# Norm scale folded into the up projection's weight rows, chunks of 1024 columns, and no weight halves on GpSimd: a hybrid decoder layer on one Trainium2 core

## The chip, the cores and the metric

The kernel runs on one core of a Trainium2 chip. The metric is the device time of one launch in microseconds (us), the median over several runs; lower is better. Five engines matter: TensorE (PE in the profile, its weight loads PEld), VectorE (DVE), ScalarE (ACT), GpSimd (POOL) and SyncE (SP), whose queue issues the weight transfers.

## The reference

One decoder layer in float32 on 256 tokens of width 2048. All of it must be computed; the part that the change touches is the last quarter of it:

```python
x = x + _rmsnorm(mixed @ w_out[layer], norm_attn_post[layer])      # 2048 -> 2048

h = _rmsnorm(x, norm_mlp_pre[layer])                               # x / rms(x) * gain
u = jnp.square(jax.nn.relu(h @ w_up[layer]))                       # 2048 -> 8192
x = x + _rmsnorm(u @ w_down[layer], norm_mlp_post[layer])          # 8192 -> 2048
```

`mixed` is what two groups of attention heads give (a dilated sliding window, and a latent attention); it is not touched.

## The kernel before

**Arithmetic.** Each float32 operand of a large product is split into two parts, `hi` and `lo`: ScalarE copies the value to the rounded type (`hi`, line 235), and another engine subtracts that from the value (`lo`, line 236). A product is then three matmuls of 128x128 by 128x512: hi·hi, hi·lo and lo·hi. The activations (`hT`, transposed, 128 tokens a block) are the stationary operand, the weights the moving one; `tok(hT[x], k, b)` is the block `b` (0 or 1) of tokens at row block `k` of 16.

**Weights.** The class `Weights` streams all weights in tiles of 128x1024 through SyncE's queue into 5 `raw` buffers; each is split into one of 8 pairs of `hi` and `lo` buffers. `get(i)` writes the instructions for tiles up to `ahead` = 6 beyond tile `i` into the program (4 while the residual below runs). The `lo` parts are on VectorE, but for three tiles of the first up chunk (`POOL_U = (3, 5, 7)`), which are on GpSimd.

**Order.** Every engine runs its instructions in the order in which the program writes them. The class `Flow` sets that order: `spend` adds a planned duration for each matmul (0.2158 us, `MM`) and transpose (0.109 us, `TR`) to a planned clock; side work is a generator (a "chain") that yields the planned delay until its next step; `pump`, called after each group of three matmuls, writes the steps that have come due. So the place of a transpose among the matmuls is fixed beforehand; if its input or its bank is late, TensorE waits there.

**From the output projection to the up projection.** When the last chunk of the output projection is done for a block `b`, `residual(b)` starts (the second block 4.0 us later in the plan, `D_SECOND`): the sum of squares, the scale `rstd_post` (GpSimd), then `update`: x += yg·rstd (line 646) and yg = x·g_pre2 (line 649) by quarters of 512 columns; after a planned 4.5 us (`D_NORM`) four steps, 1.5 us apart, each transposing a quarter of yg into a bank `ht` (2 banks, tag `tp`) and splitting it into `hT`. The factor 1/rms is not in `hT`; it comes as `rstd2[b]` when the up projection's sums are read out.

**Up projection.** 16 chunks `j` of 512 columns; each has 8 weight tiles of two row blocks (`K2`), and per tile and block 6 matmuls. The first chunk takes 7 tiles for block 0 first, then the same 7 for block 1 (`APART[1]` = 7), all else alternates between the blocks. A chunk has two accumulators (one 512-column bank per block, out of 4 with the tag `acc`). When a block's accumulator is complete, ScalarE writes r = relu(acc·rstd2) (line 739) into one of 2 buffers `r`, and a chain `up_evac` follows:

```python
    def up_evac(j, b, r):
        yield D_UP + b * 0.7                       # D_UP = 2.0
        t = tp_bank(f"rt{j}_{b}")                  # tag tp, 2 banks
        for k in range(4):
            transpose(t[:, k * P:(k + 1) * P], r[:, k * P:(k + 1) * P])
        nc.scalar.activation(uT[j][:, :, b * P:(b + 1) * P], t.rearrange("p (k s) -> p k s", k=4), AF.Square)
```

The delay counts from the first `pump` after the chain was started. A tile of `r` is free for the next one when its four transposes are done; a bank of `tp` when line 714 (uT) has read it.

**Down projection.** 16 groups of 4 row blocks with tiles of 1 x 1024 columns and 8 accumulators (all banks), then the last norm and the output.

Of the kernel before, what the change touches and what calls it, by code (L numbers as in the profile page):

```python
# [26 lines left out]
P = 128  # L27
# [43 lines left out]

RAW_BUFS, W_BUFS, W_AHEAD, AHEAD_NORM = 5, 8, 6, 4
POOL_U = (3, 5, 7)

APART = (5, 7)

# [62 lines left out]
class Weights:  # L142


    def __init__(self, nc, pool, split, bufs, ahead):
        self.nc, self.pool, self.split_fn = nc, pool, split
        self.bufs, self.limit, self.ahead = bufs, bufs, ahead
        self.specs, self.tiles, self.done, self.on_pool = [], [], [], set()

    def plan(self, src, nk, n):  # L150
        self.specs.append((src, nk, n))
        self.done.append(False)
        return len(self.specs) - 1

    def emit(self, upto):
        upto = min(upto, self.done.index(False) + self.limit, len(self.specs))
        while len(self.tiles) < upto:
            i = len(self.tiles)
            src, nk, n = self.specs[i]
            raw = self.pool.tile([P, CW], F32, tag="raw", bufs=RAW_BUFS, name=f"raw{i}")  # L160
            hi = self.pool.tile([P, CW], F32R, tag="hi", bufs=self.bufs, name=f"hi{i}")
            lo = self.pool.tile([P, CW], F32R, tag="lo", bufs=self.bufs, name=f"lo{i}")
            w = nk * n

            def v(t):
                return t[:, :w].rearrange("p (k n) -> p k n", k=nk)

            self.nc.sync.dma_start(out=v(raw), in_=src.rearrange("(k p) n -> p k n", p=P))
            cuts = [(k * n, (k + 1) * n) for k in range(nk)] if i < FINE else [(0, w)]
            for o, e in cuts:  # L170
                self.split_fn(hi[:, o:e], lo[:, o:e], raw[:, o:e], i in self.on_pool)
            self.tiles.append((v(hi), v(lo)))

    def get(self, i):
# [26 lines left out]
def layer(nc, tc, io):  # L201
    flow = Flow()

    def pool(name, side, **kw):
        return tc.alloc_tile_pool(name=name, bufs=1, side=side, **kw)

    con = pool("con", "left")
    con.tile([P, 32], F32, name="con_pad")
    xp = pool("xp", "left")
    wp = pool("wp", "left")  # L210
    ps = tc.alloc_tile_pool(name="ps", bufs=1, space=PSUM)
# [18 lines left out]
    def transpose(out, a):  # L230
        nc.tensor.transpose(out, a, ident)  # L231
        flow.spend(TR)

    def split(hi, lo, src, pool=False):
        nc.scalar.activation(hi, src, AF.Copy)  # L235
        (nc.gpsimd if pool else nc.vector).tensor_tensor(out=lo, in0=src, in1=hi.bitcast(F32), op=OP.subtract)  # L236

    def split_gain(hi, lo, src, g):
        nc.scalar.activation(hi, src, AF.Copy, scale=g)
# [4 lines left out]
        return t[:, k, b * P:(b + 1) * P]  # L244

    weights = Weights(nc, wp, split, W_BUFS, W_AHEAD)


    w_in, K2 = io["w_in"], [2] * (KD // 2)
# [14 lines left out]
    ch_o = [Chunk(weights, io["w_out"], n * 512, 512, K2, plan=False) for n in range(4)]  # L264
    for n, m in ((0, 6), (1, 6), (0, 2), (1, 2), (2, 8), (3, 8)):
        ch_o[n].plan(m)
    ch_u = [Chunk(weights, io["w_up"], j * 512, 512, K2) for j in range(FF // 512)]
    weights.on_pool.update(ch_u[0].tiles[t][0] for t in POOL_U)
    down = []
    for g in range(FF // 512):  # L270
        down.append({(c, kk): weights.plan(io["w_down"][(4 * g + kk) * P:(4 * g + kk + 1) * P, c * CW:(c + 1) * CW], 1, CW)
# [52 lines left out]
    mixT = [mix.tile([P, HA + HB, S], F32R, name=f"mixT_{w}") for w in ("hi", "lo")]  # L324
    xT = [pa.tile([P, KD, S], F32R, name=f"xT_{w}") for w in ("hi", "lo")]
    pa.tile([P, 104], F32, name="pa_pad")
    gcol = con.tile([P, 8], F32, name="gcol")
    neg_half = con.tile([P, 1], F32, name="neg_half")
    nc.gpsimd.memset(neg_half, -0.5)
    ident = con.tile([P, P], F32, name="ident")  # L330
# [305 lines left out]

    def residual(b):

        po, yg, g_pre2, hT = late["po"], late["yg"], late["g_pre2"], late["hT"]
        nc.vector.reduce_sum(ssr[b][:, 0:1], ssy[b], axis=mybir.AxisListType.X)  # L640
        r = rstd_of(ssr[b][:, 0:1], 1, D, f"post{b}")

        def update(ns):
            cs = [slice(n * 512, (n + 1) * 512) for n in ns]
            for c in cs:
                nc.vector.scalar_tensor_tensor(out=xs[b][:, c], in0=yg[b][:, c], scalar=r, in1=xs[b][:, c],
                                               op0=OP.mult, op1=OP.add)
            for c in cs:
                nc.vector.tensor_tensor(out=yg[b][:, c], in0=xs[b][:, c], in1=g_pre2[:, c], op=OP.mult)

        update((0, 1))
        yield D_NORM
        for n in range(4):
            t = tp_bank(f"ht{n}{b}")
            for k in range(4):
                transpose(t[:, k * P:(k + 1) * P], yg[b][:, n * 512 + k * P:n * 512 + (k + 1) * P])
            tv = t.rearrange("p (k s) -> p k s", k=4)
            if n in (0, 1):
                update((n + 2,))
            split(hT[0][:, 4 * n:4 * n + 4, b * P:(b + 1) * P], hT[1][:, 4 * n:4 * n + 4, b * P:(b + 1) * P], tv)  # L660
            parts[b] += 1
            yield D_HT
        for n in range(4):
            c = slice(n * 512, (n + 1) * 512)
            junk = po.tile([P, 512], BF16, tag="junk", bufs=1, name=f"junkx{n}{b}")
            nc.scalar.activation(junk, xs[b][:, c], AF.Square, accum_out=ssx[b][:, n:n + 1])
            yield 0.5
        nc.vector.reduce_sum(ssr[b][:, 1:2], ssx[b], axis=mybir.AxisListType.X)
        rstd2[b] = rstd_of(ssr[b][:, 1:2], 1, D, f"pre2{b}")
        if b == NB - 1:  # L670
            weights.ahead = W_AHEAD
# [9 lines left out]
    for ns in ((0, 1), (2,), (3,)):  # L681
        if len(ns) == 2:
            order = [(c, t, b) for ts in (range(6), range(6, 8)) for c in range(2) for t in ts for b in range(NB)]
        else:
            order = [(0, t, b) for t, b in in_order(8, (0, APART[0] if ns == (3,) else 0))]
        for c, b, acc in proj(mixT, [ch_o[n] for n in ns], f"o{ns[0]}", order, heads_done):
            n = ns[c]
            if not late:
                flow.finish(*pair_chain)
                pb.release()  # L690
                lat.release()
                hp = pool("hp", "left")
                late["hT"] = [hp.tile([P, KD, S], F32R, name=f"hT_{w}") for w in ("hi", "lo")]
                po = late["po"] = pool("po", "right")
                for nm, g in (("g_post", "norm_attn_post"), ("g_pre2", "norm_mlp_pre")):
                    late[nm] = po.tile([P, D], F32, name=nm)
                    nc.sync.dma_start(out=late[nm], in_=io[g].partition_broadcast(P).rearrange("p o d -> p (o d)"))
                late["yg"] = [po.tile([P, D], F32, name=f"yg{b}") for b in range(NB)]
            out_evac(n, b, acc[0])
            if n == 3:  # L700
                weights.ahead = AHEAD_NORM
                res[b] = flow.start(residual(b), b * D_SECOND)
                flow.pump()
# [12 lines left out]
    def split_u(g):  # L716
        if g == 0:
            uh, ul = [wp.tile([P, CW], F32R, tag=w, bufs=W_BUFS, name=f"u{w}0").rearrange("p (k s) -> p k s", k=4)
                      for w in ("hi", "lo")]
        else:  # L720
            uh, ul = [dpl["dp"].tile([P, 4, S], F32R, tag=f"u{w}", bufs=2, name=f"u{w}{g}") for w in ("hi", "lo")]
        split(uh.rearrange("p k s -> p (k s)"), ul.rearrange("p k s -> p (k s)"), uT[g].rearrange("p k s -> p (k s)"))
        return uh, ul

    evac = []
    for j in range(16):
        if j == 15:
            weights.limit -= 1
            u_next = split_u(0)
        order = [(0, t, b) for t, b in in_order(8, (APART[1] if j == 0 else 0, 0))]  # L730
        for _, b, acc in proj(hT, [ch_u[j]], f"u{j}", order, h_done):
            if not uT:
                flow.finish(*res)
                po.release()
                mix.release()
                up = pool("up", "right")
                uT += [up.tile([P, 4, S], F32, name=f"uT{i}") for i in range(16)]
            r = up.tile([P, 512], F32, tag="r", bufs=2, name=f"r{j}_{b}")
            nc.scalar.activation(r, acc[0], AF.Relu, scale=rstd2[b])  # L739
            evac.append(flow.start(up_evac(j, b, r)))  # L740
    u_last = evac[-2:]

    y = [[None] * 4 for _ in range(NB)]
    for b in range(NB):
# [96 lines left out]
def arrays_of(inputs):  # L841

    a = {n: np.ascontiguousarray(inputs[n][0]) for n in ("x", "w_in", "w_uq", "w_ukv", "w_out", "w_up", "w_down")}
    a["xt"] = np.ascontiguousarray(np.concatenate([a["x"], inputs["norm_attn_pre"]]).T)
    a["pos"] = np.ascontiguousarray(inputs["positions"].reshape(NB, P).T)
    a["gains"] = np.ascontiguousarray(np.concatenate(
        [inputs[n].reshape(-1, P) for n in ("q_latent_norm", "kv_latent_norm")]).T)
    for n in ("norm_attn_post", "norm_mlp_pre", "norm_mlp_post"):
        a[n] = np.ascontiguousarray(inputs[n])
    a["consts"] = shape_constants()  # L850
    return a
# [20 lines left out]
```

## Time and profile before

| | us |
|---|---|
| median of 3 runs | 1086.17 (1086.08 to 1087.11) |
| the profiled execution, its own time | 1086.03 |
| span in its profile, first to last instruction | 1084.2 |
| what lies around the span | 1.83 |
| TensorE busy in the span | 1069.1 (99%) |
| VectorE, ScalarE, GpSimd busy | 567.6, 526.5, 15.2 |
| mean granted TensorE clock | 0.996 of full speed |

Times in the profile count from the span's start. In rows of the timeline the columns are start, length, engine, line, operation, output<-input, form and count, and in brackets the engine's idle time before it and what ended that. Rows of the chain have start, length and what ran. Groups have busy time in us and the mean of one in ns. TensorE's matmuls are pipelined and their ends are modelled, so it is their starts that tell the pace.

### The profile page before, as it was taken

Reading aid. Unit: us, or ns where it says so; the run is one execution under the profiler, and the core shown is the slowest. Engines: PE = TensorE matmul, PEld = TensorE weight load, DVE = VectorE, ACT = ScalarE, POOL = GpSimd, SP = SyncE. Lnnn points to the kernel's source line nnn. Section 1 sums busy time; section 2 is a strip of 40 time slices with the busy share of each in tenths; the row PEclk is TensorE's granted clock in tenths of the full one; section 3 lists DMA queues with packets and bytes.
Section 4 is the critical chain, followed back from the end, with each engine's and each line's share of the span. In section 5 each row is a group of like instructions: output and inputs, shape, how many; then the busy total and the mean of one; then the engine's idle time right before and its main releaser. Section 6 shows DMA issues by size and latency. Waiting matters only on the chain.

```text
span 1084.2 us, 13045 instructions
## 1 busy us (share of the span) xinstructions
PE 1069.1 (99%) x4978; PEld 890.7 (82%) x4978; DVE 567.6 (52%) x706; ACT 526.5 (49%) x700; POOL 15.2 (1%) x20
## 2 busy tenths in 40 slices
PE   9999999999999899999999999999999999999996
PEld 6888899888888688888888888888888888888885
DVE  6486447477554863444434444345544454445444
ACT  6665446556453564544445444454444444444441
POOL 0000000000000300000000000000000000000000
PEclk9999999999999999999999999999999999999998
DMA  9885446454275375566655666546555556555532
GB/s 306 296 273 154 149 135 212 145 171 161 93 278 186 98 252 175 175 197 191 189 180 170 195 197 181 189 166 209 194 194 192 194 193 232 193 194 194 194 119 79
DMA packets 89967, 203.09 MB, mean 187 GB/s; under 512 B 6832, under 2 KB 11440, under 8 KB 89648
## 3 DMA queue, kind: packets, MB, share of 16 engines
q1 hardware_dynamic: 89472, 201.89, 57.4%
q8 instruction: 39, 0.64, 0.3%
q10 hardware_dynamic: 432, 0.37, 0.1%
q14 instruction: 24, 0.20, 0.0%
HBM read 200.13 MB, written 2.10 MB: 187 GB/s over the span
## 4 chain that ended last, share of the span: by engine, by line
PE 97%; issue 1%; DMA 1%; DVE 1%; ACT 0%; POOL 0%; DVEq 0%; POOLq 0%; ACTq 0%
PE y L227 32%; PE acc_u L227 32%; PE acc_o L227 8%; PE acc_k L227 4%; PE acc_v L227 4%; PE acc_q L227 4%; PE acc_ckv L227 2%; PE acc_ukv L227 2%; PE acc_cq L227 2%; PE acc_uq L227 2%; PE rt L231 1%; PE sc_b L227 1%; PE sc_a L227 0%; PE o_b L227 0%; PE o_a L227 0%
## 5 line engine op out<-in xcount | busy, mean ns | idle before, releaser
L236 DVE TENSOR_TENSOR lo<-raw,hi 128x1024 fp32r<-128x1024 f32 (+3 forms) x378 | 447.2, 1189 | 443.4 <-ACT hi L235 443.0
L235 ACT ACTIVATE hi<-raw 128x1024 fp32r<-128x1024 f32 (+3 forms) x381 | 387.9, 1026 | 345.9 <-PE y L227 180.1
L227 PE MATMUL acc_u<-hi,hT_hi 128*128 128x512 f32 x512 | 203.2, 397 | 0.0
L227 PE MATMUL acc_u<-hi,hT_lo 128*128 128x512 f32 x512 | 199.8, 390 | 0.0
L227 PE MATMUL acc_u<-lo,hT_hi 128*128 128x512 f32 x512 | 199.8, 390 | 0.0
L227 PE MATMUL y<-hi,uhi 128*128 128x512 f32 x512 | 199.4, 389 | 0.0
L227 PE MATMUL y<-lo,uhi 128*128 128x512 f32 x512 | 199.2, 389 | 0.0
L227 PE MATMUL y<-hi,ulo 128*128 128x512 f32 x512 | 160.2, 389 | 0.0
L227 PEld LDWEIGHTS acc_u<-hi,hT_lo 128*128 128x128 f32 x512 | 96.4, 188 | 20.5
L227 PEld LDWEIGHTS y<-lo,uhi 128*128 128x128 f32 x512 | 96.1, 188 | 20.0
L227 PEld LDWEIGHTS y<-hi,ulo 128*128 128x128 f32 x512 | 96.1, 188 | 19.9
L227 PEld LDWEIGHTS y<-hi,uhi 128*128 128x128 f32 x512 | 96.1, 188 | 19.9
L227 PEld LDWEIGHTS acc_u<-lo,hT_hi 128*128 128x128 f32 x512 | 96.5, 189 | 18.9
L227 PEld LDWEIGHTS acc_u<-hi,hT_hi 128*128 128x128 f32 x512 | 96.5, 188 | 18.8
L227 PE MATMUL acc_o<-hi,mixT_hi 128*128 128x512 f32 x128 | 51.9, 405 | 0.0
L227 PE MATMUL acc_o<-hi,mixT_lo 128*128 128x512 f32 x128 | 50.2, 392 | 0.0
L227 PE MATMUL acc_o<-lo,mixT_hi 128*128 128x512 f32 x128 | 49.9, 390 | 0.0
L739 ACT ACTIVATE r<-acc_u,rstd_pre 128x512 f32<-128x512 f32 x32 | 21.9, 687 | 53.5 <-PE acc_u L227 53.5
L227 PEld LDWEIGHTS acc_o<-hi,mixT_lo 128*128 128x128 f32 x128 | 24.0, 188 | 5.5 <-DVE mixT_lo L236 0.4
L227 PEld LDWEIGHTS acc_o<-hi,mixT_hi 128*128 128x128 f32 x128 | 24.1, 188 | 4.6 <-ACT mixT_hi L235 0.2
L227 PEld LDWEIGHTS acc_o<-lo,mixT_hi 128*128 128x128 f32 x128 | 24.1, 188 | 4.5
L227 PE MATMUL acc_q<-hi,xT_hi 128*128 128x512 f32 x64 | 26.8, 418 | 0.8 <-ACT hi L235 0.8
(192 smaller groups left out, 1009.5 us busy)
## 6 DMA issues: line engine op xcount, KB each, us to landing
raw<-in_w_up SPq DMA_DIRECT2D x128, 512.0 KB, 4.2
raw<-in_w_down SPq DMA_DIRECT2D x128, 512.0 KB, 4.5
raw<-in_w_in SPq DMA_DIRECT2D x55, 512.0 KB, 4.9
raw<-in_w_out SPq DMA_DIRECT2D x32, 512.0 KB, 4.2
raw<-in_w_in SPq DMA_DIRECT2D x16, 288.0 KB, 2.8
raw<-in_w_ukv SPq DMA_DIRECT2D x8, 512.0 KB, 4.8
raw<-in_w_uq SPq DMA_DIRECT2D x8, 384.0 KB, 3.4
x<-in_x SPq DMA_DIRECT2D x8, 256.0 KB, 6.8
```

Of the source, the lines that this page charges most:

```text
L227: nc.tensor.matmul(out, a, b, start=start, stop=stop)
L231: nc.tensor.transpose(out, a, ident)
L235: nc.scalar.activation(hi, src, AF.Copy)
L236: (nc.gpsimd if pool else nc.vector).tensor_tensor(out=lo, in0=src, in1=hi.bitcast(F32), op=OP.subtract)
L739: nc.scalar.activation(r, acc[0], AF.Relu, scale=rstd2[b])
```

## The change

- The gain `norm_mlp_pre` is no longer multiplied into the tokens (line 649 goes, and so do the tile `g_pre2` and its load). It comes with the small table `gcol` (16 more columns), one value per row of `w_up`, and `split_gain` applies it while a tile of `w_up` is split: ScalarE's copy takes it as `scale`, and VectorE's `lo` becomes (raw·g) − hi. The transposes `ht` read `xs` itself.
- A tile of `w_up` is now one row block by 1024 columns, and the up projection has 8 chunks of 1024 columns: four accumulators a chunk (block × half), taken in turn from six banks (four `acc`, two `at`). A chunk's last row block hands over both halves of a block at once, so each block starts two chains `up_evac`.
- No `lo` part is on GpSimd.

```diff
-POOL_U = (3, 5, 7)
...
-    def plan(self, src, nk, n):
-        self.specs.append((src, nk, n))
+    def plan(self, src, nk, n, gain=None):
+        self.specs.append((src, nk, n, gain))
...
-                self.split_fn(hi[:, o:e], lo[:, o:e], raw[:, o:e], i in self.on_pool)
+                self.split_fn(hi[:, o:e], lo[:, o:e], raw[:, o:e], g)
...
-    def split(hi, lo, src, pool=False):
+    def split(hi, lo, src, g=None):
+        if g is not None:
+            return split_gain(hi, lo, src, g)
         nc.scalar.activation(hi, src, AF.Copy)
-        (nc.gpsimd if pool else nc.vector).tensor_tensor(out=lo, in0=src, in1=hi.bitcast(F32), op=OP.subtract)
+        nc.vector.tensor_tensor(out=lo, in0=src, in1=hi.bitcast(F32), op=OP.subtract)

     def split_gain(hi, lo, src, g):
         nc.scalar.activation(hi, src, AF.Copy, scale=g)
         nc.vector.scalar_tensor_tensor(
             out=lo, in0=src, scalar=g, in1=hi.bitcast(F32), op0=OP.mult, op1=OP.subtract)
...
-    ch_u = [Chunk(weights, io["w_up"], j * 512, 512, K2) for j in range(FF // 512)]
-    weights.on_pool.update(ch_u[0].tiles[t][0] for t in POOL_U)
+    wide_u = [[weights.plan(io["w_up"][k * P:(k + 1) * P, j * CW:(j + 1) * CW], 1, CW, gcol[:, 8 + k:9 + k])
+               for k in range(KD)] for j in range(FF // CW)]
...
             for c in cs:
                 nc.vector.scalar_tensor_tensor(out=xs[b][:, c], in0=yg[b][:, c], scalar=r, in1=xs[b][:, c],
                                                op0=OP.mult, op1=OP.add)
-            for c in cs:
-                nc.vector.tensor_tensor(out=yg[b][:, c], in0=xs[b][:, c], in1=g_pre2[:, c], op=OP.mult)
...
-                transpose(t[:, k * P:(k + 1) * P], yg[b][:, n * 512 + k * P:n * 512 + (k + 1) * P])
+                transpose(t[:, k * P:(k + 1) * P], xs[b][:, n * 512 + k * P:n * 512 + (k + 1) * P])
...
-    for j in range(16):
-        if j == 15:
-            weights.limit -= 1
-            u_next = split_u(0)
-        order = [(0, t, b) for t, b in in_order(8, (APART[1] if j == 0 else 0, 0))]
-        for _, b, acc in proj(hT, [ch_u[j]], f"u{j}", order, h_done):
...
-            r = up.tile([P, 512], F32, tag="r", bufs=2, name=f"r{j}_{b}")
-            nc.scalar.activation(r, acc[0], AF.Relu, scale=rstd2[b])
-            evac.append(flow.start(up_evac(j, b, r)))
-    u_last = evac[-2:]
+    turn = 0
+    for j in range(FF // CW):
+        accs = {}
+        for bn in ((b, n) for b in range(NB) for n in range(2)):
+            accs[bn] = (acc_bank if turn % 6 < 4 else at_bank)(f"acc_u{j}_{bn[0]}{bn[1]}")
+            turn += 1
+        for k, b in in_order(KD, (APART[1] if j == 0 else 0, 0)):
+            if (j, k, b) == (FF // CW - 1, KD // 2, 0):
+                weights.limit -= 1
+                u_next = split_u(0)
+            wh, wl = weights.get(wide_u[j][k])
+            h_done(k, b)
+            for n in range(2):
+                c = slice(n * 512, (n + 1) * 512)
+                for i, (x, w) in enumerate(((0, wh), (0, wl), (1, wh))):
+                    mm(accs[b, n], tok(hT[x], k, b), w[:, 0, c], k == 0 and i == 0, k == KD - 1 and i == 2)
+                flow.pump()
+            if b == NB - 1:
+                weights.free(wide_u[j][k])
+            if k == KD - 1:
...
+                for n in range(2):
+                    r = up.tile([P, 512], F32, tag="r", bufs=2, name=f"r{j}_{b}{n}")
+                    nc.scalar.activation(r, accs[b, n], AF.Relu, scale=rstd2[b])
+                    evac.append(flow.start(up_evac(2 * j + n, b, r)))
+    u_last = evac[-4:]
...
-        [inputs[n].reshape(-1, P) for n in ("q_latent_norm", "kv_latent_norm")]).T)
-    for n in ("norm_attn_post", "norm_mlp_pre", "norm_mlp_post"):
+        [inputs[n].reshape(-1, P) for n in ("q_latent_norm", "kv_latent_norm", "norm_mlp_pre")]).T)
+    for n in ("norm_attn_post", "norm_mlp_post"):
```

More of the change, by code (lines that the diff above doesn't have):

```diff
@@ L147, in __init__ @@
         self.bufs, self.limit, self.ahead = bufs, bufs, ahead
-        self.specs, self.tiles, self.done, self.on_pool = [], [], [], set()
-    def plan(self, src, nk, n):
-        self.specs.append((src, nk, n))
+        self.specs, self.tiles, self.done = [], [], []
+    def plan(self, src, nk, n, gain=None):
+        self.specs.append((src, nk, n, gain))
         self.done.append(False)
@@ L158, in emit @@
             i = len(self.tiles)
-            src, nk, n = self.specs[i]
+            src, nk, n, g = self.specs[i]
             raw = self.pool.tile([P, CW], F32, tag="raw", bufs=RAW_BUFS, name=f"raw{i}")
@@ L207, in layer @@
     con = pool("con", "left")
-    con.tile([P, 32], F32, name="con_pad")
+    con.tile([P, 16], F32, name="con_pad")
     xp = pool("xp", "left")
@@ L246, in layer @@
     weights = Weights(nc, wp, split, W_BUFS, W_AHEAD)
+    gcol = con.tile([P, 8 + KD], F32, name="gcol")
     w_in, K2 = io["w_in"], [2] * (KD // 2)
@@ L326, in layer @@
     pa.tile([P, 104], F32, name="pa_pad")
-    gcol = con.tile([P, 8], F32, name="gcol")
     neg_half = con.tile([P, 1], F32, name="neg_half")
@@ L637, in residual @@
     def residual(b):
-        po, yg, g_pre2, hT = late["po"], late["yg"], late["g_pre2"], late["hT"]
+        po, yg, hT = late["po"], late["yg"], late["hT"]
         nc.vector.reduce_sum(ssr[b][:, 0:1], ssy[b], axis=mybir.AxisListType.X)
@@ L694, in layer @@
                 po = late["po"] = pool("po", "right")
-                for nm, g in (("g_post", "norm_attn_post"), ("g_pre2", "norm_mlp_pre")):
-                    late[nm] = po.tile([P, D], F32, name=nm)
-                    nc.sync.dma_start(out=late[nm], in_=io[g].partition_broadcast(P).rearrange("p o d -> p (o d)"))
+                late["g_post"] = po.tile([P, D], F32, name="g_post")
+                nc.sync.dma_start(out=late["g_post"],
+                                  in_=io["norm_attn_post"].partition_broadcast(P).rearrange("p o d -> p (o d)"))
                 late["yg"] = [po.tile([P, D], F32, name=f"yg{b}") for b in range(NB)]
@@ L725, in layer @@
     evac = []
-    for j in range(16):
-        if j == 15:
-            weights.limit -= 1
-            u_next = split_u(0)
-        order = [(0, t, b) for t, b in in_order(8, (APART[1] if j == 0 else 0, 0))]
-        for _, b, acc in proj(hT, [ch_u[j]], f"u{j}", order, h_done):
[L732 to L737, printed above, removed]
-            r = up.tile([P, 512], F32, tag="r", bufs=2, name=f"r{j}_{b}")
-            nc.scalar.activation(r, acc[0], AF.Relu, scale=rstd2[b])
-            evac.append(flow.start(up_evac(j, b, r)))
-    u_last = evac[-2:]
+    turn = 0
[18 more added lines that the diff above has]
+            if k == KD - 1:
+                if not uT:
+                    flow.finish(*res)
+                    po.release()
+                    mix.release()
+                    up = pool("up", "right")
+                    uT += [up.tile([P, 4, S], F32, name=f"uT{i}") for i in range(16)]
+                for n in range(2):
[3 more added lines that the diff above has]
+    u_last = evac[-4:]
     y = [[None] * 4 for _ in range(NB)]
```

## The prediction

> **What bounds the kernel now.** I read the page first (engines, chain), then the chain in order of time, then the starts of TensorE's matmuls around the two places that the change touches, and last the other engines' timeline there.
>
> ```profile
> PE 1069.1 (99%) x4978; PEld 890.7 (82%) x4978; DVE 567.6 (52%) x706; ACT 526.5 (49%) x700; POOL 15.2 (1%) x20
> PE 97%; issue 1%; DMA 1%; DVE 1%; ACT 0%; POOL 0%; DVEq 0%; POOLq 0%; ACTq 0%
> ...
> 390.59 20.44 PE acc_u L227 x90
> ...
> 733.24 337.35 PE y L227 x1488
> ```
>
> TensorE is the bound: 97% of the chain. One matmul of the up projection takes 20.44/90 = 0.227 us, one of the down projection 337.35/1488 = 0.227. Change or not, the up projection has 1536 of them: 16 chunks × 8 tiles × 2 blocks × 6 before, 8 × 16 × 2 × 6 after. The down projection already reads halves of 1x1024 tiles, the new shape of the w_up tiles, at the same pace, so I cost the matmuls themselves at nothing. What can change is where TensorE stands still. Before, that is one place, the seam from the output to the up projection. The page's own time for this execution is 1086.03, its span 1084.2, so 1.83 lies around it; the median of the runs shown is 1086.17, 0.14 above. I add differences to the execution and then 0.14.
>
> TensorE's starts at the seam (timeline, one engine):
>
> ```profile
> 357.19 0.40 PE L227 MATMUL acc_u<-hi,hT_lo 128*128 128x512 f32 x1
> 358.53 0.66 PE L231 MATMUL ht<-ident,yg 128*128 128x128 f32 x4 [0.94 <-DVE hT_lo L236]
> ...
> 364.94 0.39 PE L227 MATMUL acc_u<-hi,hT_lo 128*128 128x512 f32 x1
> 369.27 1.09 PE L231 MATMUL ht<-ident,yg 128*128 128x128 f32 x4 [3.94 <-DVE yg L649]
> 372.47 0.60 PE L231 MATMUL ht<-ident,yg 128*128 128x128 f32 x4
> ```
>
> Two waits, both for VectorE: 358.53 − 357.19 − 0.23 = 1.11 us, and 369.27 − 364.94 − 0.23 = 4.10. Behind the second, one set of transposes and six matmuls take 372.47 − 369.27 = 3.20. The same set takes 1.83 later on (412.70 − 410.87, rows below), so 1.37 more is lost; the granted clock says why:
>
> ```profile
> 357.00:364.00 7.00, 6.06 (x29) 4.79 (x28) 6.97 (x8) 5.94 (x12) 2.39 (x1) 1.00 0.39 104
> 370.00:373.00 3.00, 3.00 (x13) 2.48 (x12) 2.93 (x5) 0.60 (x1) 0.98 (x1) 0.64 0.09 33
> ```
>
> The clock was 0.64 in the three us behind the long wait, and stayed 1.00 around the short one. Together the seam costs 1.11 + 4.10 + 1.37 = 6.58 us. Why VectorE is late there:
>
> ```profile
> 349.75 1.42 DVE L646 SCALAR_TENSOR_TENSOR x<-yg,rstd_post,x 128x512 f32<-128x512 f32 x2 [0.66 <-POOL rstd_post L318]
> 354.20 2.40 POOL L236 TENSOR_TENSOR lo<-raw,hi 128x1024 fp32r<-128x1024 f32 x1 [4.49 <-ACT hi L235]
> 354.28 2.87 DVE L646 SCALAR_TENSOR_TENSOR x<-yg,rstd_post,x 128x512 f32<-128x512 f32 x1
> 358.31 2.39 POOL L236 TENSOR_TENSOR lo<-raw,hi 128x1024 fp32r<-128x1024 f32 x1 [1.71 <-ACT hi L235]
> 358.99 2.79 DVE L236 TENSOR_TENSOR lo<-raw,hi 128x1024 fp32r<-128x1024 f32 x1
> 362.90 1.21 DVE L236 TENSOR_TENSOR lo<-raw,hi 128x1024 fp32r<-128x1024 f32 x1
> 364.97 2.34 POOL L236 TENSOR_TENSOR lo<-raw,hi 128x1024 fp32r<-128x1024 f32 x1
> 365.03 3.49 DVE L646 SCALAR_TENSOR_TENSOR x<-yg,rstd_post,x 128x512 f32<-128x512 f32 x2 [0.67 <-POOL rstd_post L318]
> 368.44 1.28 DVE L649 TENSOR_TENSOR yg<-x,g_pre 128x512 f32<-128x512 f32 x2
> ```
>
> An x update of 0.71 us (1.42 for two) takes 2.87 under GpSimd's first `lo`; a `lo` of 1.21 takes 2.79 under the second; two updates take 3.49 under the third. In all three, VectorE's instruction ends only after GpSimd's. That is 2.16 + 1.58 + 2.07 = 5.8 us of VectorE held up.
>
> **The change at the seam.** Removed: these 5.8 us, and eight multiplies by g_pre2 (0.64 each by the last row). Added: three `lo` parts on VectorE, and a scale in each split:
>
> ```profile
> L239 ACT ACTIVATE xT_hi<-xraw 128x256 fp32r<-128x256 f32 x16 | 7.2, 500 | 1.2 <-DMA xraw<-in_xt 1.1
> L240 DVE SCALAR_TENSOR_TENSOR xT_lo<-xraw,xT_hi 128x256 fp32r<-128x256 f32 x16 | 6.9, 480 | 2.3 <-ACT xT_hi L239 2.3
> L236 DVE TENSOR_TENSOR mixT_lo<-o_a,mixT_hi 128x256 fp32r<-128x256 f32 x8 | 3.4, 424 | 7.2 <-ACT mixT_hi L235 7.2
> L235 ACT ACTIVATE mixT_hi<-o_a 128x256 fp32r<-128x256 f32 x8 | 3.1, 384 | 9.8 <-PE o_a L227 9.8
> ```
>
> With the scale a 128x256 `lo` takes 0.480 instead of 0.424 and a `hi` 0.500 instead of 0.384. If that surcharge is fixed, a 128x1024 `lo` is 1.21 + 0.06 = 1.27 and a `hi` 1.05 + 0.12 = 1.17; if it grows with the length, it is four times as much, 1.43 and 1.51. I take the first (the nearest rows have no longer form). A tile has 12 × 0.227 = 2.72 us of matmuls, so either value is hidden in the steady up projection, and costs something only where VectorE or ScalarE is waited for.
>
> Block 0: without hold-up the update of 354.28 ends near 356.2 even with a `lo` of 1.27 ahead of it, its quarter of hT_lo near 356.9; TensorE comes to the waiting transposes at 357.4. The wait of 1.11 goes. Block 1: VectorE is busy without a break from 354.28 to the sum of squares at 364.0. It loses 2.16 + 1.58 there and one multiply (0.6), gains two `lo` (2.54) and two surcharges (0.12): the update starts some 1.7 earlier than at 365.03, near 363.3, its first quarter ends near 364.0, and the transposes no longer wait for line 649. TensorE comes to them at 364.94 + 0.23 − 1.11 = 364.06. So the wait of 4.10 goes, and with it the slow clock (1.37). What is late next: the third new `lo` now lies in VectorE's queue between block 1's two updates (to 364.6) and its hT_lo. That `lo` (1.27), two small steps of rstd2 (0.4), one update (0.7), hT_lo (0.7) end near 367.6; TensorE, after six matmuls and two sets of transposes, needs it near 366.8: about 0.85 us. Seam: 6.58 − 0.85 = 5.7 us gained; from below 4.0 (if the dear surcharge and late updates leave 2.6), from above 6.58.
>
> The load of g_pre2 (1 MB on SP's queue) goes, and the table gcol on ScalarE's queue grows from 8 to 24 columns; no wait on TensorE ends with either, so nothing for both. Tiles, their order and buffers in SP's queue are the same.
>
> **The change at the chunk ends.** One boundary before (ScalarE, then TensorE):
>
> ```profile
> 407.73 0.69 ACT L739 ACTIVATE r<-acc_u,rstd_pre 128x512 f32<-128x512 f32 x1 [3.08 <-PE acc_u L227]
> 409.08 0.69 ACT L739 ACTIVATE r<-acc_u,rstd_pre 128x512 f32<-128x512 f32 x1 [0.67 <-PE acc_u L227]
> 409.67 1.05 ACT L235 ACTIVATE hi<-raw 128x1024 fp32r<-128x1024 f32 x1
> 411.50 0.60 ACT L714 ACTIVATE uT<-rt 128x512 f32<-128x512 f32 x1 [0.78 <-PE rt L231]
> 412.00 1.05 ACT L235 ACTIVATE hi<-raw 128x1024 fp32r<-128x1024 f32 x1
> ...
> 410.87 0.60 PE L231 MATMUL rt<-ident,r 128*128 128x128 f32 x4
> 411.22 0.48 PE L227 MATMUL acc_u<-hi,hT_hi 128*128 128x512 f32 x1
> ...
> 412.70 0.60 PE L231 MATMUL rt<-ident,r 128*128 128x128 f32 x4
> ```
>
> Block 0's r starts at 407.73, its transposes 3.14 later, 15 matmuls after its last one (groups of three by the planned clock: due at 0.65 + 2.0 = 2.65, written at 3.24), block 1's six matmuls behind that. Nothing waits: two r, two banks rt.
>
> After, a boundary has four r in two buffers and four rt in two banks. By the same planned clock both chains of block 0 come due at 2.65 and are written at 3.24; that moves the clock to 4.11, block 1's two are due at 1.94 + 2.7 = 4.64 and are written after the next group, at 4.76. TensorE's order is then: 15 matmuls, rt 00 and rt 01, three matmuls, rt 10 and rt 11. ScalarE's order: r 00, r 01, r 10, r 11, one `hi`, uT 00, uT 01, uT 10, uT 11. Counted from block 0's last r (0 = 407.73):
>
> - rt 00 starts at 3.14 and is done for its readers at 3.14 + (411.50 − 410.87) = 3.77. Only then is a buffer free for r 10. The whole ScalarE queue stands behind it.
> - r 10 from 3.77, r 11 from 4.36 (0.59 apart, 409.08 to 409.67), the `hi` from 4.95 (its weights are there), uT 00 from 6.02 (1.05 and 0.12 for the scale, less the 0.10 by which one instruction starts ahead of the last one's listed end), done at 6.62 (0.60).
> - TensorE comes to rt 10 at 3.14 + 0.4 + 1.15 = 4.69 (1.83 less three matmuls, and the other rt). Its bank is rt 00's, free at 6.62. It waits 1.93. For rt 11 it waits another 0.15 (uT 01 ends 0.50 later; TensorE needs 0.35 per rt).
>
> So 2.08 us at each of seven boundaries between chunks: 14.6 us. Behind TensorE's head wait the next matmuls, and nothing can take over. From below 1.9 (a `hi` with less than 0.12 on top): 13.3; from above 2.4 (full lengths, a slow first matmul behind the wait): 16.8. The eighth chunk ends in the down projection, where `pump` comes only every 12 matmuls: block 1's rt follow 2.72 us of matmuls behind block 0's, and uT 00 is done by then; nothing. The accumulators don't wait: the next chunk opens on the two spare banks, then on block 0's, read by 0.7 and needed from 2.4.
>
> Sum: 14.6 − 5.7 = +8.9; 1086.03 + 8.9 + 0.14 = 1095.1 on the scale of the runs. The bounds give 13.3 − 6.6 = +6.7 to 16.8 − 4.0 = +12.8: 1092.9 to 1099.0.
>
> What the trace doesn't show is whether a wait of 2 us lowers the clock: 0.94 did not, 3.94 did. It is nearer to the shorter one, so I take no loss. The Trainium skill ("TensorE: Matmul & The Clock Gate", Part 1) says that the clock is halved after a whole idle window of about 3.4 us; the trace's two waits agree, and by that rule 2 us cost no clock. The same page (section "A second HAM failure mode: psum-queue depth-cycling") says that short idles which recur as banks are cycled made the clock swing too; this speaks against the change, and no row before shows it.
>
> **The rivals.**
>
> *The clock drops at every boundary.* For it: the slow stretch behind 369.27. Against: none behind 358.53. Each of seven waits then costs 1.37 more, 9.6 in all: 1104.7. That is what the second section of that page would mean here. 0.10.
>
> *The seam keeps its wait.* If it is VectorE's work and not GpSimd's that makes it late (three more `lo`, dear scale), the 5.7 stay away: 1086.17 + 14.6 = 1100.8. Against: all three long rows lie under GpSimd's. 0.08.
>
> *Not slower: the boundaries don't wait.* One mechanism: ScalarE frees rt 00's bank before TensorE gets to rt 10. That holds if r 10 does not wait for rt 00, since ScalarE would then stand ready for uT 00 at 3.77, and end it at 4.4, ahead of 4.69. Then only the seam is left: 1086.17 − 5.7 = 1080.5. It decides from a wait under 5.7/7 = 0.8 us a boundary. For it: before, no boundary waits at all. Against: buffers, banks and order as written. 0.09.
>
> *They cancel* (waits of 0.5 to 1.1 a boundary): within 0.2%, 1084.0 to 1088.3. 0.03. This 0.2% is about what a measurement of this kernel can tell from no change.
>
> **How the numbers follow.** The forecast has 0.70, so its 1095.1 is the predicted time. Its bounds, widened by 1 us below, and up to the kept seam (1100.8) make 1092 to 1101; left out are the clock's rival, no waits, and cancelling, 0.22. Faster by over 0.2%: 0.09; within: 0.03; slower: 0.70 + 0.10 + 0.08 = 0.88.
>
> **What would show it.** Right: in TensorE's timeline seven gaps of about 2 us in the up projection, each ahead of a set of rt and released by ScalarE's uT, some 43 to 46 us apart; ScalarE idle about 3 us ahead of a r with TensorE's rt as the releaser; the waits ahead of ht gone, the first ht of block 1 near 364, updates of 0.7; chunks' matmuls at 0.227. Wrong: rt without a wait; a clock below 1.00 behind the gaps; ht still waiting; or a wait for `hi` or `lo` in the up projection, which would make the split the bound.

## The result, and the profile after

The changed kernel takes 1096.44 us (median of 6 runs, 1095.43 to 1097.54) against 1086.64 (1086.08 to 1087.65) beside it: a ratio of 1.0090, 95% interval 1.0077 to 1.0103, so 9.8 us slower. The profiled execution took 1097.54, 11.5 more than the one shown of before.

The page after (engines, chain):

```profile
PE 1072.2 (98%) x4978; PEld 891.2 (81%) x4978; DVE 567.0 (52%) x701; ACT 537.5 (49%) x700; POOL 7.0 (1%) x17
...
PE 94%; ACT 2%; DVE 1%; issue 1%; DMA 1%; POOL 0%; DVEq 0%; POOLq 0%; SPq 0%; ACTq 0%
```

TensorE has as many matmuls as before, but ScalarE now has 2% of the chain, where it had 0%. The waits by releaser say where:

```profile
ACT r L753 <- PE rt L230: 26.2, 8, 3.7
PE rt L230 <- ACT uT L713: 12.6, 7, 1.8
```

ScalarE waited eight times for transposes ahead of a read-out r, and TensorE seven times for ScalarE's uT, 1.8 us each; neither row was there before. The first of the seven places, TensorE's timeline and then ScalarE's:

```profile
404.48 1.03 PE L230 MATMUL rt<-ident,r 128*128 128x128 f32 x8
405.27 0.48 PE L226 MATMUL acc_u<-hi,hT_hi 128*128 128x512 f32 x1
405.59 0.40 PE L226 MATMUL acc_u<-lo,hT_hi 128*128 128x512 f32 x1
405.82 0.40 PE L226 MATMUL acc_u<-hi,hT_lo 128*128 128x512 f32 x1
408.04 1.14 PE L230 MATMUL rt<-ident,r 128*128 128x128 f32 x8 [1.82 <-ACT uT L713]
...
400.66 1.31 ACT L753 ACTIVATE r<-acc_u,rstd_pre 128x512 f32<-128x512 f32 x2 [2.31 <-PE acc_u L226]
405.20 1.27 ACT L753 ACTIVATE r<-acc_u,rstd_pre 128x512 f32<-128x512 f32 x2 [3.23 <-PE rt L230]
406.36 1.15 ACT L240 ACTIVATE hi<-raw,gcol 128x1024 fp32r<-128x1024 f32 x1
407.39 1.08 ACT L713 ACTIVATE uT<-rt 128x512 f32<-128x512 f32 x2
```

This is the order worked out beforehand: eight transposes of block 0, three matmuls, eight of block 1. ScalarE stands 3.23 us ahead of block 1's r, until the first rt is done, then runs two r, a hi and the first uT; TensorE stands from one matmul to the next step for 408.04 − 405.82 = 2.22, which is 1.99 more than a matmul's pace.

The seam (VectorE, then TensorE):

```profile
356.00 0.74 DVE L647 SCALAR_TENSOR_TENSOR x<-yg,rstd_post,x 128x512 f32<-128x512 f32 x1
363.65 1.42 DVE L647 SCALAR_TENSOR_TENSOR x<-yg,rstd_post,x 128x512 f32<-128x512 f32 x2 [0.67 <-POOL rstd_post L320]
364.98 1.28 DVE L241 SCALAR_TENSOR_TENSOR lo<-raw,gcol,hi 128x1024 fp32r<-128x1024 f32 x1
367.09 0.68 DVE L237 TENSOR_TENSOR hT_lo<-ht,hT_hi 128x512 fp32r<-128x512 f32 x1
...
364.36 0.39 PE L226 MATMUL acc_u<-hi,hT_lo 128*128 128x512 f32 x1
364.59 0.60 PE L230 MATMUL ht<-ident,x 128*128 128x128 f32 x4
...
367.09 0.40 PE L226 MATMUL acc_u<-lo,hT_hi 128*128 128x512 f32 x1
367.83 0.50 PE L226 MATMUL acc_u<-hi,hT_lo 128*128 128x512 f32 x1 [0.34 <-DVE hT_lo L237]
```

The updates take 0.74 and 1.42 (2.87 and 3.49 before), block 1's first transposes follow a matmul at 0.23 without a wait, and one wait is left, for the hT_lo behind the new lo: 0.74 − 0.23 = 0.51.

What had not been put into the sum: behind two of the seven waits the granted clock falls. Here is the third wait, as it ends and behind it:

```profile
500.00:503.00 3.00, 1.20 (x8) 0.72 (x7) 0.64 (x1) 2.98 (x5) 0.00 (x0) 1.00 0.00 0
503.00:506.00 3.00, 3.00 (x13) 2.55 (x13) 0.64 (x1) 2.54 (x5) 0.00 (x0) 0.59 0.39 106
506.00:509.00 3.00, 3.00 (x13) 2.44 (x12) 2.48 (x2) 1.62 (x2) 0.00 (x0) 0.84 0.34 100
```

The column ahead of the last two is the clock: 1.00, then 0.59 and 0.84.

### The profile page after: what moved, and what is told of

It reads as the page before. It is cut to its first block, busy times and chain, and to the rows that moved or that the text cites. A ratio compares the mean times of both kernels' runs of the same rounds, so it can differ in the third digit from the quotient of the medians.

```text
span 1095.8 us, 13040 instructions
## 1 busy us (share of the span) xinstructions
PE 1072.2 (98%) x4978; PEld 891.2 (81%) x4978; DVE 567.0 (52%) x701; ACT 537.5 (49%) x700; POOL 7.0 (1%) x17
## 4 chain that ended last, share of the span: by engine, by line
PE 94%; ACT 2%; DVE 1%; issue 1%; DMA 1%; POOL 0%; DVEq 0%; POOLq 0%; SPq 0%; ACTq 0%
PE y L226 31%; PE acc_u L226 31%; PE acc_o L226 8%; PE acc_k L226 4%; PE acc_v L226 4%; PE acc_q L226 4%; PE acc_ckv L226 2%; PE acc_ukv L226 2%; PE acc_cq L226 2%; PE acc_uq L226 2%; PE rt L230 1%; PE sc_b L226 1%; DMA raw<-in_w_in 1%; ACT hi L240 1%; ACT r L753 1%
## 5 line engine op out<-in xcount | busy, mean ns | idle before, releaser
L237 DVE TENSOR_TENSOR lo<-raw,hi 128x1024 fp32r<-128x1024 f32 (+3 forms) x253 | 293.0, 1165 | 260.6 <-ACT hi L236 260.2
L236 ACT ACTIVATE hi<-raw 128x1024 fp32r<-128x1024 f32 (+3 forms) x253 | 252.9, 1011 | 238.4 <-PE y L226 179.6
L241 DVE SCALAR_TENSOR_TENSOR lo<-raw,gcol,hi 128x1024 fp32r<-128x1024 f32 x128 | 163.0, 1284 | 195.9 <-ACT hi L240 195.8
L240 ACT ACTIVATE hi<-raw,gcol 128x1024 fp32r<-128x1024 f32 x128 | 146.2, 1150 | 136.8 <-PE acc_u L226 130.6
L230 PE MATMUL rt<-ident,r 128*128 128x128 f32 x128 | 18.0, 285 | 12.6 <-ACT uT L713 12.6
L230 PEld LDWEIGHTS rt<-ident,r 128*128 128x128 f32 x128 | 14.6, 142 | 17.4 <-ACT uT L713 15.7
```

Of the source, the lines that this page charges most:

```text
L237: nc.vector.tensor_tensor(out=lo, in0=src, in1=hi.bitcast(F32), op=OP.subtract)
L241: nc.vector.scalar_tensor_tensor(out=lo, in0=src, scalar=g, in1=hi.bitcast(F32), op0=OP.mult, op1=OP.subtract)
```

## The experiments

Ratios are to the kernel before, run beside each; differences in us are of medians.

**The chunks alone.** The changed kernel with the norm's gain multiplied into the tokens and the three lo parts on GpSimd again.

```diff
-               ... 1, CW, gcol[:, 8 + k:9 + k])
+               ... 1, CW, "pool" if (j, k) in ((0, 3), (0, 5), (0, 7)) else None)
+            for c in cs:
+                nc.vector.tensor_tensor(out=yg[b][:, c], in0=xs[b][:, c], in1=g_pre2[:, c], op=OP.mult)
```

> The chunks of 1024 columns alone: the norm's gain is multiplied into the tokens again and three lo parts are on GpSimd, as before. My theory (the waits at the chunk ends and the seam are independent costs): the seam's waits of 1.11 and 4.10 us come back, the seven waits ahead of block 1's rt stay at about 1.9 to 2.0 us each, so 1086.2 + 13.8 + 1.6 to 3.9 for one or two stretches of slow clock behind them = 1101 to 1104. Rival (the longer hi with the scale makes the waits): a hi of 1.05 instead of 1.15 leaves waits under 1 us, 1093 to 1096.

Measured: 1100.28 (ratio 1.0124, 1.0109 to 1.0139), 13.3 more than before. The seam is the old one again:

```profile
354.10 2.88 DVE L645 SCALAR_TENSOR_TENSOR x<-yg,rstd_post,x 128x512 f32<-128x512 f32 x1
364.85 3.49 DVE L645 SCALAR_TENSOR_TENSOR x<-yg,rstd_post,x 128x512 f32<-128x512 f32 x2 [0.67 <-POOL rstd_post L318]
...
412.05 0.40 PE L226 MATMUL acc_u<-hi,hT_lo 128*128 128x512 f32 x1
414.18 1.15 PE L230 MATMUL rt<-ident,r 128*128 128x128 f32 x8 [1.73 <-ACT uT L713]
...
414.00:417.00 3.00, 2.82 (x16) 2.42 (x17) 0.96 (x2) 2.74 (x6) 0.00 (x0) 1.00 0.36 85
```

The waits at the chunk ends stay, so they belong to the chunks and not to the scale. They are 0.1 shorter than in the changed kernel (2.10 to 2.13 between starts against 2.20 to 2.22), by the hi of 1.05 instead of 1.15. The expected range was missed by 0.7 on the low side: in the profiled execution none of the seven waits was followed by a slow clock (1.00 in the last row, behind the first).

**The gain without the chunks.** 16 chunks of 512 columns as before, scaled rows, no lo on GpSimd.

```diff
-    wide_u = [[weights.plan(..., 1, CW, gcol[:, 8 + k:9 + k]) ...
+    ch_u = [Chunk(weights, io["w_up"], j * 512, 512, K2, gain=gcol[:, 8:8 + KD]) for j in range(FF // 512)]
```

> The gain on the rows of w_up and no lo on GpSimd, but 16 chunks of 512 columns with tiles of two row blocks, each row block split by itself (two hi and two lo of 512 columns a tile). My theory: the seam's gain without the waits at the chunk ends, 6.0 us less than before: 1080 to 1081, and no wait ahead of rt. Rival (the scaled split is too slow for the up projection): TensorE waits for hi or lo within the chunks, 1086 or more.

Measured: 1081.04 (ratio 0.9944, 0.9928 to 0.9961), 5.9 less than before. From 340 us to the end of the up projection one wait is left, 0.88 between two starts at 367.4, the same hT_lo. 256 splits of half a tile (0.72 on ScalarE, 0.75 on VectorE) made TensorE wait nowhere.

**GpSimd alone.** The kernel before with one edit.

```diff
-POOL_U = (3, 5, 7)
+POOL_U = ()
```

> The kernel before with one edit: no lo part on GpSimd; the multiply by g_pre2 stays. My theory (GpSimd's lo holds VectorE up): the wait of 1.11 goes; the updates of block 1 start 1.4 us earlier and take 1.42 instead of 3.49, the transposes wait about 1.7 us and a later one 0.9; no slow clock. 6.58 - 2.6 = 4.0 less: 1082. Rival (VectorE's own work makes the seam late): three more lo of 1.15 us on it, 1086 to 1089.

Measured: 1082.56 (ratio 0.9962, 0.9947 to 0.9977), 4.4 less.

```profile
363.81 1.41 DVE L646 SCALAR_TENSOR_TENSOR x<-yg,rstd_post,x 128x512 f32<-128x512 f32 x2 [0.67 <-POOL rstd_post L318]
365.14 1.28 DVE L649 TENSOR_TENSOR yg<-x,g_pre 128x512 f32<-128x512 f32 x2
...
364.16 0.39 PE L227 MATMUL acc_u<-hi,hT_lo 128*128 128x512 f32 x1
365.97 0.63 PE L231 MATMUL ht<-ident,yg 128*128 128x128 f32 x4 [1.42 <-DVE yg L649]
```

Three more lo on VectorE, and it is earlier all the same: the two updates take 1.41 instead of 3.49. What GpSimd had was no help but a hold-up. The multiply still costs a wait of 1.58 (365.97 − 364.16 − 0.23), and the later one for hT_lo is 1.14 (369.85 − 368.48 − 0.23). The previous run, with the gain on the rows, has 0.65 there (0.88 − 0.23) and no other, so the gain on the rows is worth about 2.1 by these waits; by the medians it is 1.5, with that run's other splits in it.

**A hi less in the queue.** The changed kernel; the tile written into the program at a chunk's first row block is written at its second.

```diff
-            wh, wl = weights.get(wide_u[j][k])
+            wh, wl = weights.tiles[wide_u[j][k]] if j and k == 0 else weights.get(wide_u[j][k])
```

> The changed kernel with one edit: the weight tile that is written into the program at a chunk's first row block is written at its second, so no hi stands between r 11 and uT 00 on ScalarE. My theory (ScalarE's queue r 10, r 11, hi, uT 00 is the wait): each of the seven waits shrinks by the hi's 1.03, from 1.99 to about 0.95, 7.2 us in all, and as 0.94 was followed by no slow clock before, the slow stretches (1.6 to 3.9 us) go too: 1085 to 1088, with runs at one level. Rival (TensorE waits for something else that ends with uT): no change, 1095 to 1098.

Measured: 1087.09 (10 runs, 1086.45 to 1087.61; ratio 1.0001, 0.9992 to 1.0010).

```profile
405.55 1.27 ACT L753 ACTIVATE r<-acc_u,rstd_pre 128x512 f32<-128x512 f32 x2 [3.23 <-PE rt L230]
406.70 1.09 ACT L713 ACTIVATE uT<-rt 128x512 f32<-128x512 f32 x2
...
406.17 0.40 PE L226 MATMUL acc_u<-hi,hT_lo 128*128 128x512 f32 x1
407.36 1.14 PE L230 MATMUL rt<-ident,r 128*128 128x128 f32 x8 [0.79 <-ACT uT L713]
```

uT follows r directly, and the wait is 1.19 − 0.23 = 0.96, shorter by the hi's 1.03. All seven are so (1.16 to 1.19), none with a slow clock behind it. The chunks' waits and the seam's gain now cancel.

**A hi more.** At the first row block two tiles are written instead of one.

```diff
             wh, wl = weights.get(wide_u[j][k])
+            if j and k == 0:
+                weights.emit(wide_u[j][k] + 8)
```

> The changed kernel with one edit: at a chunk's first row block two weight tiles are written into the program instead of one, so that two hi stand between r 11 and uT 00. My theory (the wait is ScalarE's queue, and the clock falls the more often the longer TensorE stands): each of the seven waits grows by 1.03, from 1.99 to 3.0, 7.2 us in all, and slow stretches of about 1.6 us follow more than two of them: 1096.4 + 7.2 + 0 to 8 = 1104 to 1112. Rival (slow stretches come at a fixed number a launch, whatever the wait): two of them, 1103.6 to 1105.6.

Measured: 1113.62, four runs from 1104.94 to 1119.18 (ratio 1.0219, 1.0167 to 1.0271).

```profile
455.83 2.18 ACT L240 ACTIVATE hi<-raw,gcol 128x1024 fp32r<-128x1024 f32 x2
...
455.32 0.40 PE L226 MATMUL acc_u<-hi,hT_lo 128*128 128x512 f32 x1
458.55 1.97 PE L230 MATMUL rt<-ident,r 128*128 128x128 f32 x8 [2.83 <-ACT uT L713]
...
459.00:460.00 1.00, 1.00 (x7) 1.00 (x6) 0.50 (x1) 0.29 (x1) 0.00 (x0) 0.50 0.72 98
460.00:466.00 6.00, 6.00 (x20) 4.80 (x19) 1.28 (x1) 2.71 (x4) 0.00 (x0) 0.62 0.68 227
```

The wait is 3.23 − 0.23 = 3.00, 1.01 longer, as worked out. The clock is at 0.50 while the transposes still run and 0.62 over the next six us. In this profile, of the slowest execution, all seven waits are followed by matmuls 0.42 to 0.58 apart, 7 to 10 of them each. The spread of 14 us between runs fits a number that differs from one execution to the next, but only this one was profiled. Three of the four runs lie above the rival's range of two stretches. The expected top of 1112 was too low, because such a stretch costs up to 2.8 here: from the third wait to the fourth it is 51.2 us, against 47.4 + 1.0 without.

**Block 1's r in memory of their own**, in the halves of uT[15], which is unused until the last chunk.

```diff
-                    r = up.tile([P, 512], F32, tag="r", bufs=2, ...)
+                    if b and j < FF // CW - 1:
+                        r = uT[15].rearrange("p k s -> p (k s)")[:, n * 512:(n + 1) * 512]
+                    else:
+                        r = up.tile([P, 512], F32, tag="r", bufs=2, ...)
```

> The changed kernel with one edit: r 10 and r 11 are written into the two halves of uT[15], which stands unused until the last chunk, so that they don't wait for block 0's transposes (the last chunk as before). Still two banks for four rt. My theory (the wait begins with r 10, which stands at the head of ScalarE's queue until rt 00 is done): uT 00 ends by 4.5 on the clock of the prediction, TensorE comes at 4.69; waits of 0 to 0.2: 1080 to 1081.5. Rival (two banks are too few for four sets of transposes): the waits of 2 us stay, 1095 to 1098.

Measured: 1079.93 (ratio 0.9936, 0.9920 to 0.9953), 7.0 less than before.

```profile
405.00 1.03 PE L230 MATMUL rt<-ident,r 128*128 128x128 f32 x8
...
406.34 0.39 PE L226 MATMUL acc_u<-hi,hT_lo 128*128 128x512 f32 x1
406.57 1.04 PE L230 MATMUL rt<-ident,uT 128*128 128x128 f32 x8
...
405.64 1.09 ACT L713 ACTIVATE uT<-rt 128x512 f32<-128x512 f32 x2 [0.75 <-PE rt L230]
```

With the same two banks and the same places for rt, TensorE goes from a matmul to rt in 0.23: no wait. ScalarE stands ready for uT. So two banks are enough; it was the r without a buffer that held ScalarE's queue.

**Block 1's rt further back**, with the two r buffers as they are; and the same with one more edit in the residual.

```diff
-        yield D_UP + b * 0.7
+        yield D_UP + b * 3.4
```

> The changed kernel with one edit: the delay of block 1's chains is D_UP + 3.4 instead of D_UP + 0.7, which puts rt 10 and rt 11 twelve matmuls (2.7 us) further back. r 10 still waits for rt 00. My theory (it is the place of rt 10 against the end of uT 00): TensorE comes to rt 10 at 7.6 on the clock of the prediction, uT 00 ends at 6.6: no waits, no slow clock, 1080 to 1081.5. Rival (ScalarE's stop at r 10 itself costs, by late hi): waits for hi in the chunks, above 1084.

> As the one before, and in the residual the split of a quarter of hT is written ahead of the update of the next quarter but one. My theory: hT_lo of block 1's first quarter then ends 0.7 us earlier and the wait of 0.5 us at 367.1 goes, 0.5 less than the run before: about 1080. Rival: the later updates delay the next transposes by as much: no difference.

Measured: 1079.51 (ratio 0.9938, 0.9923 to 0.9953) and 1079.12 (0.9929, 0.9914 to 0.9944). The first of the two:

```profile
405.01 1.27 ACT L753 ACTIVATE r<-acc_u,rstd_pre 128x512 f32<-128x512 f32 x2 [3.23 <-PE rt L230]
...
408.36 0.39 PE L226 MATMUL acc_u<-hi,hT_lo 128*128 128x512 f32 x1
408.59 1.03 PE L230 MATMUL rt<-ident,r 128*128 128x128 f32 x8
```

In it, ScalarE still stands 3.23 us ahead of block 1's r, and it costs nothing, since TensorE comes to block 1's rt fifteen matmuls behind block 0's instead of three; this is the other remedy for the same wait. In the second, the wait of 0.51 for hT_lo is gone and one of 0.18 ahead of block 1's first transposes is left. The two runs' intervals overlap, so those 0.4 us are not settled by the times. Both beat the kernel before and the changed one.

**The changed kernel again**, three times, for its two levels of time.

> The changed kernel unchanged, for its two levels of time (1095.4 to 1095.5 and 1097.3 to 1097.5). My theory (behind some of the seven waits the clock falls, once or twice in a launch): the profile of a run at the lower level has one slow stretch fewer than the one at hand, which has two (behind the third and the seventh wait); every stretch costs 1.6 to 2.0 us. Rival (the levels come from the start or the end of the launch): the same two stretches at either level.

> The changed kernel, one more profile. If the two levels of time (about 1095.5 and 1097.4) come from the number of slow stretches, a time below 1096 goes with one of them and a time above 1096.9 with two.

> The same once more: one slow stretch below 1096, two above 1096.9.

Measured: 1097.17 as the median of four (1095.73 to 1098.14), then 1097.57 and 1096.74. Each of the three profiles (at 1096.96, 1097.57 and 1096.74) has two slow stretches, as the first one had (at 1097.54). They are behind different waits: third and seventh first, then second and sixth, second and sixth, first and fourth. The 1096.74 lies between the two levels. No execution near 1095.5 was caught in a profile. That the lower level has one stretch fewer fits its distance (1.9 against 1.6 for a stretch) but stays open.

## Why the prediction was right, step by step

The forecast was 1095.1, the median is 1096.44; the mechanisms were those named, with one term put at nothing that was not nothing.

- *The seam.* Forecast 6.58 − 0.85 = 5.7 gained. Measured 6.58 − 0.51 = 6.1. That the hold-up by GpSimd was the cause, and not VectorE's own work, is shown by the run with that edit alone; the rival of a kept seam falls. The wait for hT_lo behind the third new lo came as named, 0.3 shorter.
- *The chunk ends.* Forecast 2.08 each, of which 1.93 ahead of rt 10. Measured 1.99 there; a plain pair of 512-column chunks took (543.97 − 407.73)/3 = 45.4 before, by block 0's r six chunks apart,

```profile
543.97 0.69 ACT L739 ACTIVATE r<-acc_u,rstd_pre 128x512 f32<-128x512 f32 x1 [3.08 <-PE acc_u L227]
```

  and a chunk of 1024 takes 47.4 after (first wait to second, 405.82 to 453.26, the gaps without a slow clock): 2.0 each, 14.0 in all, against 14.6. Against the same chunk without its wait (45.3, from rt at 405.00 to rt at 450.30 in the run with block 1's r apart) it is 2.1: 1.99 ahead of rt 10 and 0.11 in the eight transposes behind it (1.14 instead of 1.03), for which the forecast had 0.15. The forecast had the gaps 43 to 46 us apart; 43.6 of matmuls and 2.0 of wait leave out some 1.8 for the 16 transposes of a chunk. The queue was tested link by link: a hi less and a hi more moved the wait by 1.03 and 1.01, and taking away either the missing buffer or the early place of rt removed it whole. The rival "not slower" named the right condition: when r 10 does not wait for rt 00 there are no waits. It put that at 5.7 less than before; the run gave 7.0 less, of which 6.1 are the seam's. The other 0.9 is no larger than the spread of that kernel's and of before's runs (1.4 and 1.7); the chunk that takes 45.3 instead of 45.4 would make 0.8 of it over seven chunks, and why it does is open.
- *The clock.* The prediction took no loss behind a wait of 2 us; this is the term that was mis-sized, and a clock below 1.00 behind the gaps was one of its own signs of being wrong. It judged by the length of the wait alone; the last section shows that 2 us is just at the edge. Two stretches cost 1.6 each, 3.2 in the profiled execution: the spacing 500.67 to 549.66 is 48.99 instead of 47.4, and from the end of the seventh wait to the down projection it is 43.42 (694.03 to 737.45), against 41.84 in the first repeat, where the clock stayed up (695.06 to 736.90). The rival with a drop behind all seven was too much. With the two the sum is 14.0 + 3.2 − 6.1 = 11.1, and the profiled executions differ by 11.5; 0.55 of that comes ahead of the up projection, whose first matmul starts at 355.46 instead of 354.91. That the median came within 1.4 of the forecast is partly luck: the chunk ends were put 0.6 too dear and the seam's gain 0.4 too small, which made up for part of the clock.
- The Trainium skill ("TensorE: Matmul & The Clock Gate", Part 1) has the clock halved after a whole idle window of about 3.4 us. Here it fell behind waits of 1.99, so the measurement decides against reading that as a safe length. The same page's section "A second HAM failure mode: psum-queue depth-cycling", on short idles that recur as banks are cycled, agrees with what the runs show for waits of 1.99 and 3.00; behind those of 0.96 and 1.88, which recur as well, the clock stayed up.

## What to carry to other kernels

When an output tile is made twice as wide, count the staging buffers and banks of its read-out, not only its accumulators: four read-outs in two buffers put a transpose between two instructions of an in-order queue, and TensorE, the bound, then waited for all that stood behind it in that queue. Such a wait can be removed at either end, with memory for the blocked write or with a later place for what reads it; a few lines or one did it here and turned 1.0090 into 0.9936 or 0.9938. Work put on an idle engine is not free when it holds up a busy one: three subtractions on GpSimd cost 4.4 us net (2.5 to 5.8 by the interval).

## What the runs showed of the hardware that was not expected

Behind a short wait of TensorE the clock may fall or not, and the length of the wait alone doesn't decide. In the profiles here it fell behind 0 of 7 waits of 0.96 us, 0 of 7 of 1.88, 2 of 7 of 1.99 (in each of four executions), and in the slowest execution 7 of 7 of 3.00. Which of the equal waits is hit changes from one execution to the next, and the traces show on what that depends. In each of the thirteen, the granted clock changes only at whole steps of 3.41 us, counted through the whole execution. In the profiled execution of the changed kernel the two slow stretches are one step long each (503.56 to 506.97 and 694.70 to 698.11), 56 steps apart. The step ahead of the first, the slow one, and the next:

```profile
500.15:503.56 3.41, 1.61 (x11) 1.06 (x10) 1.20 (x1) 3.15 (x6) 0.00 (x0) 1.00 0.00 0
503.56:506.97 3.41, 3.41 (x11) 2.83 (x10) 1.03 (x2) 3.21 (x4) 0.00 (x0) 0.50 0.49 154
506.97:510.38 3.41, 3.41 (x16) 2.81 (x16) 2.33 (x3) 1.21 (x2) 0.00 (x0) 1.00 0.51 166
```

The number behind the comma is TensorE's busy time: 1.61 of 3.41. In the thirteen traces, every step at full clock with less than 1.59 of it was followed by a slow step, none with more than 1.61, and of the 18 between 8 were. A wait of 1.99 (1.80 idle in the profile) leaves 1.6 when it lies inside one step, which is the edge itself, and more when it reaches into the next; one of 1.88 left at least 1.68. This is read from the traces; no run was made to test it. It also means that 7 of 7 is no rate for waits of 3.00: a chunk with such a wait and its slow stretch takes 51.2 us, which is 15 steps, so behind the second wait every further one lay at the same place of a step.

The spread of times is 14 us with the waits of 3.00; with those of 1.99 it is 2.7, with those of 0.96 it is 1.2, and the kernel before, without any, has 2.0.
